# Two-layer hybrid decoder trunk: pairs of feed-forward chunks multiplied by seven block products

## The chip, the cores and the metric

The kernel runs on one NeuronCore of a Trainium2 chip. The metric is the device time of one execution in microseconds. The kernel before took 992.43 us (median of 3 runs, 991.97 to 992.92).

## The reference

The input x is 256 tokens of 1024 values in fp32. Two layers are computed. Each is a feed-forward block, a token mixer and a second feed-forward block, each behind an RMS norm and added to x (the feed-forward blocks with a factor 0.5). The mixer of layer 0 is a causal convolution module (pointwise, gate, 31-tap depthwise, layer norm, pointwise), that of layer 1 is stick-breaking attention with 16 heads of 64. One RMS norm ends it. The part that the change concerns is the feed-forward block:

```python
def swiglu_ffn(h, w_in, w_out):          # h: 256 x 1024, w_in: 1024 x 5632, w_out: 2816 x 1024
    gate, up = jnp.split(h @ w_in, 2, axis=-1)
    return (jax.nn.silu(gate) * up) @ w_out

x = x + 0.5 * swiglu_ffn(rms_norm(x, g[0]), ffn_w_in[i, 0], ffn_w_out[i, 0])
x = x + mixer(rms_norm(x, g[1]))
x = x + 0.5 * swiglu_ffn(rms_norm(x, g[2]), ffn_w_in[i, 1], ffn_w_out[i, 1])
```

There are four such blocks, called the first to the fourth below: the first and the second lie around the convolution, the third and the fourth around the attention.

## The kernel before, in words

**Numbers.** Every large product is made of three matmuls of a reduced fp32 type (fp32r). An operand is split into "hi", a cast copy made by ScalarE, and "lo", the difference that VectorE computes (`split`, L147 to L149); `mm3` (L177) then adds hi x hi, hi x lo and lo x hi into one PSUM bank. Weights arrive by DMA in a raw buffer (pool `rawp`, three of them, each 8 KB a partition) and are split into a pair of hi and lo buffers (pool `ring`, six pairs). `load_w` (L151) does this in pieces of 1024 elements a partition. All weight loads are issued on SP's queue.

**A feed-forward block** (`ffn`, L263) runs over 11 chunks of 256 hidden columns. For a chunk j the kernel loads two weight tiles of w_in (four of the eight 128-row slices each; 256 gate and 256 up columns side by side) and one row tile of w_out (`load_rows`, "v"), computes the up-projection and the gate, and one chunk later adds the chunk's down-projection to four PSUM banks that collect the block's output (`V`, L309, 12 matmuls of 512 columns for each half t of the tokens). There are two forms of the up-projection:
- U (`u_mm`, L227, with `gate`, L267, and `A`, L277): the tokens are the stationary operand and 512 weight columns move. 24 matmuls of 512 columns for each half of 128 tokens. The result has tokens in the partitions; sigmoid and two products follow, then two transposes by TensorE (`A`) and a split.
- C (`C`, L287, with `u_cm`, L235): 128 weight columns are stationary, and the tokens move, hi and lo side by side (512 columns) for the weights' hi and 256 columns for their lo. The result has hidden columns in the partitions and needs no transposes.

The norm's gain is multiplied into the transposed x (`gain`, L203, tile `xg`, 512 elements, tag "B"), which is then split into `xT` (`split_x`, `boundary`, L216). The norm's factor of a token, rstd, is not in `xT`: U's gate multiplies by it, and C multiplies by a row of it (`rrow`, L294 on VectorE, L298 on GpSimd). Chunk 0 of a block, and chunks 0 and 1 of the first, are in the form U, the rest in the form C.

**Order.** The framework in which the kernel is written plans each engine's order before the run: it takes the instructions by program order, as they become ready in its own estimate, and gives out the buffers of a pool as they come free. Each engine then runs its list in order. The opening (`start`, L804) and the convolution (L584 to L647) have their orders written out by hand on TensorE, ScalarE, VectorE and SP. Small work tiles share tags: thirteen buffers of tag "A", four of "B", four each of "H" and "L" for the down-projection's operand.

## Time and profile before

| | before |
|---|---|
| median of 3 runs | 992.43 us (991.97 to 992.92) |
| profiled execution | 992.41 us, span 990.6 us |
| TensorE matmuls | 977.4 us busy (99%), 5658 of them |
| VectorE | 722.3 us busy (73%), 1127 instructions |
| ScalarE | 514.0 us busy (52%), 873 |
| GpSimd | 132.8 us busy (13%), 165 |
| granted TensorE clock | 0.997 of 2.4 GHz (mean) |
| moved from HBM | 171.10 MB, 174 GB/s over the span |

Busy times are sums of recorded durations, and the records of successive instructions of one engine overlap a little: the distance between two starts is shorter than a duration. PE is TensorE's matmul queue, DVE VectorE, ACT ScalarE, POOL GpSimd, SP the engine that issues most DMAs. The blocks lie at about 0 to 205, 306 to 490, 490 to 677 and 797 to 988 us of the span; the convolution is between the first two, attention from 677 to 797.

### The profile page before, as it was taken

How to read it: one execution, taken by the hardware profiler on the slowest of the kernel's cores; microseconds unless marked ns; L12 is line 12 of the kernel's file. 1: busy time of each engine (PE TensorE's matmuls, PEld its weight loads, DVE VectorE, ACT ScalarE, POOL GpSimd, SP SyncE). 2: the span in 40 equal slices, each digit the busy share in tenths (PEclk: the TensorE clock that was granted, in tenths of full speed). 3: DMA queues.
4: the chain of work that ended last, by engine and by line, in shares of the span. 5: the costliest groups of instructions: out<-in, count | busy, mean ns of one | idle time of the engine just before them, and what ended most of it. 6: DMA issues, size and time to landing. Idle time of an engine off the chain costs nothing.

```text
span 990.6 us, 14730 instructions
## 1 busy us (share of the span) xinstructions
PE 977.4 (99%) x5658; PEld 813.6 (82%) x5658; DVE 722.3 (73%) x1127; ACT 514.0 (52%) x873; POOL 132.8 (13%) x165
## 2 busy tenths in 40 slices
PE   8999999999999999999999999999999999999996
PEld 7888888886788888888888888888777688888885
DVE  5886767659869776767876767676867887767654
ACT  6664545355437555455554545454644455554532
POOL 3011111100001111111211111112100011111111
PEclk9999999999999999999999999999999999999998
DMA  7976564447736564646456565654633344646411
GB/s 256 314 242 219 193 228 148 152 125 224 226 96 223 170 229 151 227 155 216 155 192 203 171 211 165 218 152 154 205 126 130 120 153 157 230 151 223 160 43 42
DMA packets 142630, 177.17 MB, mean 179 GB/s; under 512 B 6393, under 2 KB 125792, under 8 KB 142560
## 3 DMA queue, kind: packets, MB, share of 16 engines
q1 hardware_dynamic: 142208, 175.69, 54.5%
q8 instruction: 44, 0.72, 0.3%
q10 hardware_dynamic: 352, 0.55, 0.1%
q14 instruction: 26, 0.21, 0.1%
HBM read 171.10 MB, written 1.05 MB: 174 GB/s over the span
## 4 chain that ended last, share of the span: by engine, by line
PE 92%; DVE 3%; issue 2%; ACT 1%; DMA 1%; POOL 0%; SPq 0%; POOLq 0%; ACTq 0%; DVEq 0%
PE psc L242 28%; PE psc L243 16%; PE psv L178 8%; PE psv L180 8%; PE psv L179 8%; PE psc L245 4%; PE psu L178 3%; PE psu L179 3%; PE psu L180 3%; PE pc L506 3%; DVE lo L149 2%; PE ptr L200 1%; PE pz L700 1%; DMA raw<-in_ffn_w_in_dram 1%; ACT hi L148 1%
## 5 line engine op out<-in xcount | busy, mean ns | idle before, releaser
L149 DVE TENSOR_TENSOR lo<-raw,hi 128x1024 fp32r<-128x1024 f32 (+1 forms) x358 | 398.9, 1137 | 79.4 <-ACT hi L148 79.0
L242 PE MATMUL psc<-xT,hi 128*128 128x512 f32 x1204 | 433.4, 399 | 0.1
L148 ACT CAST hi<-raw 128x1024 fp32r<-128x1024 f32 (+1 forms) x360 | 327.5, 952 | 89.4 <-PE psc L242 34.1
L243 PE MATMUL psc<-xT,lo 128*128 128x256 f32 x1376 | 358.8, 281 | 0.0
L243 PEld LDWEIGHTS psc<-xT,lo 128*128 128x128 f32 x1376 | 260.0, 189 | 15.6 <-issue 0.4
L242 PEld LDWEIGHTS psc<-xT,hi 128*128 128x128 f32 x1204 | 226.6, 188 | 49.3 <-DVE u L248 0.4
L298 POOL TENSOR_TENSOR s<-s,rrow 128x256 f32<-128x256 f32 x78 | 90.7, 1163 | 580.1 <-DVE s L297 580.1
L178 PE MATMUL psv<-hi,ah 128*128 128x512 f32 x354 | 138.2, 390 | 0.3
L179 PE MATMUL psv<-lo,ah 128*128 128x512 f32 x354 | 137.6, 389 | 0.0
L180 PE MATMUL psv<-hi,al 128*128 128x512 f32 x354 | 137.1, 389 | 0.0
L247 ACT COPY u<-psc 128x256 f32<-128x256 f32 x172 | 63.5, 369 | 130.0 <-PE psc L245 129.9
L248 DVE TENSOR_TENSOR u<-psc,u 128x256 f32<-128x256 f32 x172 | 72.5, 421 | 78.4 <-ACT u L247 77.7
L148 ACT CAST ah<-s 128x256 fp32r<-128x256 f32 x78 | 31.7, 407 | 92.2 <-DVE s L300 92.0
L179 PEld LDWEIGHTS psv<-lo,ah 128*128 128x128 f32 x354 | 66.6, 188 | 13.8
L180 PEld LDWEIGHTS psv<-hi,al 128*128 128x128 f32 x354 | 66.4, 188 | 13.8
L178 PEld LDWEIGHTS psv<-hi,ah 128*128 128x128 f32 x354 | 66.5, 188 | 13.3 <-ACT ah L148 1.4
L178 PE MATMUL psu<-hi,xT 128*128 128x512 f32 x176 | 70.2, 399 | 0.2 <-ACT hi L148 0.2
L179 PE MATMUL psu<-lo,xT 128*128 128x512 f32 x176 | 69.3, 394 | 0.8 <-DVE lo L149 0.6
L180 PE MATMUL psu<-hi,xT 128*128 128x512 f32 x176 | 68.9, 391 | 0.0
L245 PE MATMUL psc<-xT,hi 128*128 128x512 f32 x172 | 68.4, 398 | 0.0
L296 ACT ACTIVATE s<-u 128x256 f32<-128x256 f32 x78 | 32.4, 415 | 47.7 <-DVE u L294 47.7
L149 DVE TENSOR_TENSOR al<-s,ah 128x256 fp32r<-128x256 f32 x78 | 33.0, 422 | 21.1 <-ACT ah L148 20.9
(134 smaller groups left out, 800.6 us busy)
## 6 DMA issues: line engine op xcount, KB each, us to landing
raw<-in_ffn_w_in_dram SPq DMA_DIRECT2D x168, 512.0 KB, 4.6
raw<-in_ffn_w_out_dram SPq DMA_DIRECT2D x44, 1024.0 KB, 4.8
raw<-in_conv_w_pw_dram SPq DMA_DIRECT2D x16, 512.0 KB, 4.6
raw<-in_attn_w_qkv_dram SPq DMA_DIRECT2D x16, 512.0 KB, 5.1
raw<-in_ffn_w_in_dram SPq DMA_DIRECT2D x16, 256.0 KB, 5.0
raw<-in_conv_w_pw_dram SPq DMA_DIRECT2D x4, 1024.0 KB, 4.9
raw<-in_attn_w_qkv_dram SPq DMA_DIRECT2D x4, 1024.0 KB, 5.0
raw<-in_attn_w_o_dram SPq DMA_DIRECT2D x4, 1024.0 KB, 4.7
```

Source lines behind the costliest of these rows:

```text
L148: copy(hi, src)
L149: (eng or nc.vector).tensor_tensor(lo, src, hi.bitcast(F32), op=ALU.subtract)
L178: nc.tensor.matmul(ps, lh, rh, start=start, stop=False)
L179: nc.tensor.matmul(ps, lh, rl, start=False, stop=False)
L180: nc.tensor.matmul(ps, ll, rh, start=False, stop=stop)
L242: nc.tensor.matmul(ps, h, xT[:, :, k, :, :], start=k == 0, stop=False)
L243: nc.tensor.matmul(ps[:, :, 0, :], l, xT[:, :, k, 0, :], start=False, stop=False)
L245: nc.tensor.matmul(ps, h, xT[:, :, k, :, :], start=False, stop=True)
L247: nc.scalar.copy(u, ps[:, :, 1, :])
L248: nc.vector.tensor_tensor(u, ps[:, :, 0, :], u, op=ALU.add)
L296: nc.scalar.activation(a, u, AF.Sigmoid)
L298: nc.gpsimd.tensor_tensor(a, a, rrow, op=ALU.mult)
```

## The change

Pairs of chunks (ja, jb) are computed by Strassen's scheme in Winograd's form (`strassen`). The tokens (two halves t) and the contraction (two halves of four 128-row slices) make x a 2 x 2 block matrix, the contraction halves and the two chunks make w_in one. Seven products of 128 tokens x 512 contraction x 512 columns replace eight. Four of the seven weight operands are formed by subtractions in the raw buffers (`less`, in two pieces of 1024), all seven are split (`cast`). Four of the token operands are sums, formed once a block (`normalize`). The products go alternately to two PSUM banks; copies and additions (`keep`, `plus`, 512 elements each) combine them.

As the sums have to be of normalized tokens, `normalize` multiplies the kept `xg` tiles by the row of rstd, splits them into `xT` anew, and from there on the gates need no rstd (`gate_normal`; `C` leaves its two products out). A pair's results go through `gate_normal` and `A`, so that a pair needs four times two transposes.

A plan says what each chunk does: the first block UUCCUnSUUCC, the others UUnUSUSUUUU (U and C as above, n normalize, S a pair). All chunks of the second to fourth block outside of the pairs are in the form U. The waiting down-projections of the chunk before a pair are placed between its products (`later`) and after them; those of a pair come after the next chunk. The convolution's constants are loaded after the first block's chunk 8 instead of chunk 5. There are four raw buffers instead of three and ten work tiles "A" instead of thirteen, and some small tiles share buffers of other tags. The number of hi and lo buffers stays at six.

```diff
@@ -42,7 +42,7 @@
-    rawp = ctx.enter_context(tc.tile_pool(name="rawp", bufs=3))
+    rawp = ctx.enter_context(tc.tile_pool(name="rawp", bufs=4))
...
@@ -59,13 +59,12 @@
-    grow = const.tile([NG, P], F32, name="grow")
+    grow = wk.tile([NG, P], F32, tag="sg", name="grow")
-    vrow = const.tile([NV, P], F32, name="vrow")
...
@@ -215,9 +213,11 @@
 
     def boundary(t, gi):
 
+        xgs = []
         for q in range(2):
-            split_x(t, q, gain(turn_x(t, q), gi, q))
-        return *operand(t), rms_stats(t)
+            xgs.append(gain(turn_x(t, q), gi, q))
+            split_x(t, q, xgs[q])
+        return *operand(t), rms_stats(t), xgs
 
     def u_step(ps, t, k, units):
         h, l = operand(t)
...
@@ -243,7 +243,7 @@
-        u = wk.tile([P, T, P], F32, tag="A", bufs=13, name=nm("u"))
+        u = wk.tile([P, T, P], F32, tag="A", bufs=10, name=nm("u"))
...
@@ -262,15 +262,25 @@
 
     def ffn(i, f, gi, hTs, next_gi, first=None, start=None, hook=None, final=False):
         w_in, w_out = ffn_w_in[i, f], ffn_w_out[i, f]
-        act, aT = {}, {}
+        act, aT, normal, sums = {}, {}, [], []
+
+        def gate_normal(t, j, src):
+
+            s = wk.tile([P, 256], F32, tag="A", bufs=10, name=nm("s"))
+            nc.scalar.activation(s, src[:, 0:256], AF.Sigmoid)
+            nc.vector.tensor_tensor(s, src[:, 0:256], s, op=ALU.mult)
+            nc.vector.tensor_tensor(s, src[:, 256:512], s, op=ALU.mult)
+            act[t, j] = s
 
         def gate(t, j, ps):
+            if normal:
+                return gate_normal(t, j, ps)
             rstd = hTs[t][2]
-            s = wk.tile([P, 256], F32, tag="A", bufs=13, name=nm("s"))
+            s = wk.tile([P, 256], F32, tag="A", bufs=10, name=nm("s"))
             nc.scalar.activation(s, ps[:, 0:256], AF.Sigmoid, scale=rstd)
-            p = wk.tile([P, 256], F32, tag="A", bufs=13, name=nm("p"))
+            p = wk.tile([P, 256], F32, tag="A", bufs=10, name=nm("p"))
             nc.vector.scalar_tensor_tensor(p, ps[:, 0:256], rstd, s, op0=ALU.mult, op1=ALU.mult)
-            a = wk.tile([P, 256], F32, tag="A", bufs=13, name=nm("a"))
+            a = wk.tile([P, 256], F32, tag="A", bufs=10, name=nm("a"))
             nc.vector.scalar_tensor_tensor(a, ps[:, 256:512], rstd, p, op0=ALU.mult, op1=ALU.mult)
             act[t, j] = a
 
...
@@ -291,11 +301,13 @@
                 for c in range(2):
                     u = u_cm([w[:, :, c, q * P : (q + 1) * P] for w in unit] for unit in units)
                     if c == 0:
-                        nc.vector.tensor_tensor(u, u, rrow, op=ALU.mult)
-                        a = wk.tile([P, T, P], F32, tag="A", bufs=13, name=nm("s"))
+                        if not normal:
+                            nc.vector.tensor_tensor(u, u, rrow, op=ALU.mult)
+                        a = wk.tile([P, T, P], F32, tag="A", bufs=10, name=nm("s"))
                         nc.scalar.activation(a, u, AF.Sigmoid)
                         nc.vector.tensor_tensor(a, a, u, op=ALU.mult)
-                        nc.gpsimd.tensor_tensor(a, a, rrow, op=ALU.mult)
+                        if not normal:
+                            nc.gpsimd.tensor_tensor(a, a, rrow, op=ALU.mult)
                     else:
                         nc.vector.tensor_tensor(a, a, u, op=ALU.mult)
                 ah = operands.tile([P, T, P], F32R, tag="H", bufs=4, name=nm("ah"))
...
@@ -305,6 +317,106 @@
                 ls.append(al)
             for t in range(T):
                 aT[t, j] = [h[:, t, :] for h in hs], [l[:, t, :] for l in ls]
+
+        def normalize():
+
+            x11, x12, x21, x22 = (xg for t in range(T) for xg in hTs[t][3])
+            for n, xg in enumerate((x11, x12, x21, x22)):
+                t, q = divmod(n, 2)
+                nc.vector.tensor_tensor(
+                    xg, xg, rrow[:, t, :].unsqueeze(1).broadcast_to([P, 4, P]), op=ALU.mult
+                )
+                split_x(t, q, xg)
+            normal.append(True)
+
+            def operand_of(dst, a, b, op):
+                nc.vector.tensor_tensor(dst, a, b, op=op)
+                hl = wk.tile([P, 2, 4, P], F32R, tag="sk", bufs=4, name=nm("sx"))
+                split(hl[:, 0], hl[:, 1], dst)
+                return hl[:, 0], hl[:, 1]
+
+            s1 = operand_of(x22, x21, x22, ALU.add)
+            s3 = operand_of(x21, x11, x21, ALU.subtract)
+            s2 = operand_of(x11, x22, x11, ALU.subtract)
+            s4 = operand_of(x12, x12, x11, ALU.subtract)
+            sums.extend((s1, s2, s3, s4))
+
+        def strassen(ja, jb, later):
+
+            wv = w_in.rearrange("(k p) n -> p k n", p=P)
+            raw = {}
+            for h, j in ((0, ja), (0, jb), (1, jb), (1, ja)):
+                raw[h, j] = rawp.tile([P, 4, 2, 256], F32, tag="raw", name=nm("raw"))
+                for c in range(2):
+                    c0 = c * DFF + 256 * j
+                    nc.sync.dma_start(raw[h, j][:, :, c, :], wv[:, 4 * h : 4 * h + 4, c0 : c0 + 256])
+            b11, b12, b21, b22 = raw[0, ja], raw[0, jb], raw[1, ja], raw[1, jb]
+            pieces = [slice(0, 2), slice(2, 4)]
+
+            def cast(src):
+                hi, lo = (ring.tile([P, 4, 2, 256], F32R, tag=tag, name=nm(tag)) for tag in ("hi", "lo"))
+                for ks in pieces:
+                    split(hi[:, ks], lo[:, ks], src[:, ks])
+                return hi, lo
+
+            def less(dst, a, b):
+                for ks in pieces:
+                    nc.vector.tensor_tensor(dst[:, ks], a[:, ks], b[:, ks], op=ALU.subtract)
+
+            def product(ps, x, w):
+                for k in range(4):
+                    mm3(ps, x[0][:, k, :], x[1][:, k, :], w[0][:, k], w[1][:, k], k == 0, k == 3)
+
+            def old(t, q):
+                h, l = operand(t)
+                return h[:, 4 * q : 4 * q + 4, :], l[:, 4 * q : 4 * q + 4, :]
+
+            def plus(a, b, dst=None):
+                if dst is None:
+                    dst = wk.tile([P, 512], F32, tag="B", bufs=4, name=nm("sum"))
+                nc.vector.tensor_tensor(dst, a, b, op=ALU.add)
+                return dst
+
+            def keep(src):
+                dst = wk.tile([P, 512], F32, tag="B", bufs=4, name=nm("kept"))
+                nc.scalar.copy(dst, src)
+                return dst
+
+            s1, s2, s3, s4 = sums
+            px, py = (ps_u.tile([P, 512], F32, tag="u", name=nm("psp")) for _ in range(2))
+            w = cast(b11)
+            product(px, old(0, 0), w)
+            less(b11, b12, b11)
+            w = cast(b11)
+            p1 = keep(px)
+            product(py, s1, w)
+            less(b11, b22, b11)
+            w = cast(b11)
+            p5 = keep(py)
+            product(px, s2, w)
+            w = cast(b21)
+            u2 = plus(px, p1)
+            product(py, old(0, 1), w)
+            later(0)
+            less(b12, b22, b12)
+            w = cast(b12)
+            gate_normal(0, ja, plus(py, p1, p1))
+            product(px, s3, w)
+            less(b21, b21, b11)
+            w = cast(b21)
+            u3 = plus(px, u2)
+            plus(u2, p5, u2)
+            product(py, old(1, 1), w)
+            gate_normal(1, jb, plus(u3, p5, p5))
+            w = cast(b22)
+            gate_normal(1, ja, plus(py, u3, u3))
+            product(px, s4, w)
+            gate_normal(0, jb, plus(px, u2, u2))
+            A(0, ja)
+            A(1, jb)
+            later(1)
+            A(1, ja)
+            A(0, jb)
 
         def V(t, j, unit, qs=(0, 1)):
             ah, al = aT[t, j]
...
@@ -370,37 +482,70 @@
             for t in range(T)
         ]
         outs, vus = [None, None], []
-        for j in range(NJ):
-            if j == 0 and first:
-                units = first
-            elif not start or j >= lead:
-                units = load_pairs(w_in, 256 * j, DFF + 256 * j, 256, pieces=2 if j else 4)
-            if j == 0 or j >= lead:
-                vus += [load_rows(w_out, 2 * c) for c in range(len(vus), j + 1)]
-            if j == lead:
+
+        plan = list("UUCCUnSUUCC" if start else "UUnUSUSUUUU")
+        j, waiting, rrow = 0, [], None
+
+        def load_vus(last):
+            vus.extend(load_rows(w_out, 2 * c) for c in range(len(vus), last + 1))
+
+        def finish_waiting():
+            for c, t in waiting:
+                V(t, c, vus[c])
+
+        while j < NJ:
+            kind = plan.pop(0)
+            if j >= lead and rrow is None:
                 rrow = row_rstd(hTs)
-            if j < lead:
-                if not start:
+            if kind == "n":
+                normalize()
+                continue
+            if kind == "S":
+                before = waiting
+
+                def later(t):
+                    for c, tt in before:
+                        if tt == t:
+                            V(t, c, vus[c])
+
+                strassen(j, j + 1, later)
+                load_vus(j + 1)
+                waiting = [(j, 0), (j + 1, 1), (j, 1), (j + 1, 0)]
+                j += 2
+            else:
+                if j == 0 and first:
+                    units = first
+                elif not start or j >= lead:
+                    units = load_pairs(w_in, 256 * j, DFF + 256 * j, 256, pieces=2 if j else 4)
+                if j == 0 or j >= lead:
+                    load_vus(j)
+                if kind == "U":
+                    if j >= lead or not start:
+                        for t in range(T):
+                            gate(t, j, u_mm(t, units))
                     for t in range(T):
-                        gate(t, j, u_mm(t, units))
-                for t in range(T):
-                    A(t, j)
-            else:
-                C(j, units, rrow)
-            if j == NJ - 1:
-                V(0, j - 1, vus[j - 1])
-                V(1, j - 1, vus[j - 1], (0,))
-                V(0, j, vus[j])
-                finish = end_final if final else end
-                outs[0] = finish(0)
-                V(1, j - 1, vus[j - 1], (1,))
-                V(1, j, vus[j])
-                outs[1] = finish(1)
-            elif j:
-                for t in range(T):
-                    V(t, j - 1, vus[j - 1])
-            if j == 5 and hook:
+                        A(t, j)
+                else:
+                    C(j, units, rrow)
+                if j == NJ - 1:
+                    for c, t in waiting:
+                        if c < j - 1:
+                            V(t, c, vus[c])
+                    V(0, j - 1, vus[j - 1])
+                    V(1, j - 1, vus[j - 1], (0,))
+                    V(0, j, vus[j])
+                    finish = end_final if final else end
+                    outs[0] = finish(0)
+                    V(1, j - 1, vus[j - 1], (1,))
+                    V(1, j, vus[j])
+                    outs[1] = finish(1)
+                else:
+                    finish_waiting()
+                    waiting = [(j, t) for t in range(T)]
+                j += 1
+            if hook and j >= 9:
                 hook()
+                hook = None
         return outs
 
 
...
@@ -652,6 +797,8 @@
+        maskn = wk.tile([P, P], BF16, tag="sg", name="maskn")
+        identb = wk.tile([P, P], BF16, tag="sg", name="identb")
```

## Rows read from the trace of the kernel before

**Rows 1.** The page, parts 1 and 2: engine totals, granted clock in 40 slices.
```profile
PE 977.4 (99%) x5658; PEld 813.6 (82%) x5658; DVE 722.3 (73%) x1127; ACT 514.0 (52%) x873; POOL 132.8 (13%) x165
...
PEclk9999999999999999999999999999999999999998
```
**Rows 2.** Waits of TensorE's matmuls: engine, line, releaser, us in total, times, longest.
```profile
PE spare L813 <- POOL ident masks.py:199: 1.7, 1, 1.7
PE pc L506 <- issue: 1.4, 2, 0.8
```
**Rows 3.** Stretch, busy PE, PEld, DVE, ACT, POOL, clock, DMA: opening, block 2, attention, chunk.
```profile
0.00:31.60 31.60, 28.89 (x130) 23.26 (x131) 19.96 (x32) 19.48 (x33) 7.54 (x20) 1.00 0.81 270
...
306.00:490.00 184.00, 183.81 (x961) 156.18 (x960) 136.28 (x209) 99.99 (x162) 25.62 (x23) 1.00 0.59 195
...
677.00:797.00 120.00, 119.06 (x662) 91.64 (x661) 92.95 (x147) 58.62 (x119) 15.73 (x21) 1.00 0.44 141
...
584.75:601.47 16.72, 16.72 (x89) 14.32 (x88) 11.86 (x19) 8.82 (x14) 2.40 (x2) 1.00 0.59 188
```
**Rows 4.** Timeline of TensorE, that chunk: start, duration, engine, line, operation.
```profile
584.75 0.39 PE L242 MATMUL psc<-xT,hi 128*128 128x512 f32 x1
...
596.02 0.40 PE L178 MATMUL psv<-hi,ah 128*128 128x512 f32 x1
...
601.47 0.39 PE L242 MATMUL psc<-xT,hi 128*128 128x512 f32 x1
```
**Rows 5.** The same, end of the third block's U chunk and an A.
```profile
499.11 0.39 PE L178 MATMUL psu<-hi,xT 128*128 128x512 f32 x1
...
500.24 0.39 PE L180 MATMUL psu<-hi,xT 128*128 128x512 f32 x1
500.48 0.38 PE L281 MATMUL ptr<-ident,a 128*128 128x128 f32 x2
500.61 0.48 PE L242 MATMUL psc<-xT,hi 128*128 128x512 f32 x1
500.92 0.28 PE L243 MATMUL psc<-xT,lo 128*128 128x256 f32 x1
```
**Rows 6.** Timeline of VectorE, a block's boundary and a C chunk.
```profile
488.09 1.22 DVE L149 TENSOR_TENSOR lo<-raw,hi 128x1024 fp32r<-128x1024 f32 x1
489.22 0.69 DVE L332 SCALAR_TENSOR_TENSOR x<-psv,x 128x512 f32<-128x512 f32 x1
489.82 0.69 DVE L206 TENSOR_TENSOR xg<-ptr,gvec 128x512 f32<-128x512 f32 x1
...
326.80 0.42 DVE L297 TENSOR_TENSOR s<-s,u 128x256 f32<-128x256 f32 x1
327.13 1.22 DVE L149 TENSOR_TENSOR lo<-raw,hi 128x1024 fp32r<-128x1024 f32 x1
328.27 0.42 DVE L248 TENSOR_TENSOR u<-psc,u 128x256 f32<-128x256 f32 x1
328.60 1.44 DVE L149 TENSOR_TENSOR lo<-raw,hi 128x1024 fp32r<-128x1024 f32 x1
```
**Rows 7.** Groups of instructions by form: count, busy us, mean ns, idle before.
```profile
L149 DVE TENSOR_TENSOR lo<-raw,hi 128x1024 fp32r<-128x1024 f32 x280 | 347.5, 1256 | 73.8 <-ACT hi L148 73.6
```
**Rows 8.** Timeline of ScalarE in a steady chunk: two casts in a row.
```profile
364.96 2.00 ACT L148 CAST hi<-raw 128x1024 fp32r<-128x1024 f32 x2 [0.70 <-PE psv L180]
```
**Rows 9.** Waits of VectorE and ScalarE, the whole span.
```profile
DVE lo L149 <- ACT hi L148: 79.0, 83, 2.4
...
ACT hi L148 <- PE psc L242: 34.1, 36, 1.0
ACT hi L148 <- PE psv L180: 23.8, 33, 1.2
```
**Rows 10.** DMA issues: tile, queue, count, size of each, median us to landing.
```profile
raw<-in_ffn_w_in_dram SPq DMA_DIRECT2D x168, 512.0 KB, 4.6
...
lnb<-in_conv_ln_b_dram SPq DMA_DIRECT2D x1, 512.0 KB, 7.7
```

More of the change, by code (lines that the diff above doesn't have):

```diff
@@ L77, in load_vecs @@
     def load_vecs():
+        vrow = wk.tile([NV, P], F32, tag="sg", name="vrow")
         r0 = 0
@@ L122, in load_conv_consts @@
                 )
-            rowc = wk.tile([P, 32, 4], F32, tag="rowc", name="rowc")
+            rowc = wk.tile([P, 32, 4], F32, tag="B", bufs=4, name="rowc")
             nc.gpsimd.tensor_copy(rowc, rows.rearrange("p i c -> p c i"))
@@ L136, in trunk_kernel @@
     lnb = const.tile([P, D], F32, name="lnb")
-    maskn = const.tile([P, P], BF16, name="maskn")
-    identb = const.tile([P, P], BF16, name="identb")
     uid = [0]
@@ L254, in row_rstd @@
         for t in range(T):
-            rb = wk.tile([P, P], F32, tag="A", bufs=13, name=nm("rb"))
+            rb = wk.tile([P, P], F32, tag="A", bufs=10, name=nm("rb"))
             nc.gpsimd.tensor_copy(rb, hTs[t][2].broadcast_to([P, P]))
@@ L577, in conv @@
         for _ in range(KD):
-            up.append(wk.tile([P, H + T * P], F32, tag="A", bufs=13, name=nm("up")))
+            up.append(wk.tile([P, H + T * P], F32, tag="A", bufs=10, name=nm("up")))
             nc.gpsimd.memset(up[-1][:, :H], 0.0)
@@ L712, in scores @@
                 nc.scalar.activation(be, pz, AF.Sigmoid, scale=scale)
-                sc = wk.tile([P, WS], F32, tag="A", bufs=13, name=nm("scan"))
+                sc = wk.tile([P, WS], F32, tag="A", bufs=10, name=nm("scan"))
                 nc.vector.tensor_tensor_scan(
@@ L716, in scores @@
                 )
-                a = wk.tile([P, 3, P], F32, tag="A", bufs=13, name=nm("aa"))
+                a = wk.tile([P, 3, P], F32, tag="A", bufs=10, name=nm("aa"))
                 nc.vector.tensor_tensor(a[:, 0, :], be[:, 0, :], sc[:, 1 : P + 1], op=ALU.mult)
@@ L730, in transpose_a @@
                     nc.tensor.transpose(pa[:, c, :], a[:, c, :], ident)
-                aT = wk.tile([P, 3, P], F32, tag="A", bufs=13, name=nm("aT"))
+                aT = wk.tile([P, 3, P], F32, tag="A", bufs=10, name=nm("aT"))
                 nc.vector.tensor_copy(aT, pa)
@@ L846, in start @@
             pts = [turn_x(0, q) for q in range(2)]
-            xgs = [gain(pts[q], 0, q) for q in range(2)]
+            first_xgs = [gain(pts[q], 0, q) for q in range(2)]
             for q in range(2):
-                split_x(0, q, xgs[q])
+                split_x(0, q, first_xgs[q])
             keep_busy(8)
@@ L867, in start @@
             rstds.append(rms_stats(1))
-            hTs.extend((*operand(t), rstds[t]) for t in range(T))
+            hTs.extend((*operand(t), rstds[t], (first_xgs, xgs)[t]) for t in range(T))
             mm(0, (1, 3), (0, 4))
```

## The prediction

> **What bounds the kernel now.** I read the page's engine totals first, then the waits of the matmul engine, the busy time by stage, and the timelines of TensorE, VectorE and ScalarE inside one steady chunk. TensorE is busy 977.4 of 990.6 us at full granted clock [rows 1]. It hardly waits: the largest wait behind the opening one is 1.4 us [rows 2]. In a whole block it idles 0.2 of 184 us, and in one steady chunk of 16.72 us not at all, while VectorE is busy 11.86 us and ScalarE 8.82 us of it [rows 3]. So whatever takes matmul time away shortens the run, as long as VectorE, the next engine, still delivers its operands in time. Both sides have to be counted.
>
> **What the pairs remove from TensorE.** A C chunk runs its up-projection from 584.75 to 596.02, 11.27 us, and its down-projection (24 matmuls of 512 columns) to 601.47, 5.45 us, 0.227 each [rows 4]. In the U form the same 512-column matmuls follow each other at 1.13/5 = 0.226 us; two fp32 transposes take 0.13 us and make the next matmul 0.31 instead of 0.23 long, 0.21 us for each A in all [rows 5]. I use 0.2265 us per matmul.
> - A pair now: 2 x 11.27 = 22.54 us of up-projection. After: 7 products x 4 slices x 3 matmuls = 84 x 0.2265 = 19.03, plus 4 A's x 0.21 = 0.84, together 19.87 us. Saved: 2.67 us a pair. The down-projection stays at 10.9 us.
> - There are 1 + 2 + 2 + 2 = 7 pairs: -18.7 us.
> - Other chunks go from C to U: three in the first block, six in each of the others, 21 in all. U costs 48 x 0.2265 + 2 x 0.21 = 11.29 us, so +0.02 each, +0.4 us.
> Sum on TensorE: -18.3 us, if no wait arises.
>
> **What the change puts on VectorE.** Back to back, a 1024-element operation starts 1.13 to 1.14 us after the one before, a 512 one 0.60, a 256 one 0.33 to 0.34; their durations in the record are 1.22, 0.69 and 0.42 [rows 6]. A pair has 14 "lo" halves of seven operands, 8 subtractions that form four of the weight operands, 4 "lo" halves of two row tiles, 7 additions of 512 and 12 operations of 256 (eight in the gates, four in the A's): 26 x 1.14 + 7 x 0.60 + 12 x 0.34 = 37.9 us. Two C chunks need 12 x 1.14 + 24 x 0.34 = 21.8. TensorE has 19.9 + 10.9 = 30.8 us for a pair, so inside one VectorE is short; over a block it is not: 7 U chunks x 8.9 + 2 x 37.9 + 16 x 0.60 for the normalization = 148 us, against 7 x 16.7 + 2 x 30.8 = 179 on TensorE. The question is whether VectorE's lead carries it over the pairs.
>
> The lead that a pair needs: up to the seventh operand's first half VectorE has 22 x 1.14 + 5 x 0.60 + 4 x 0.34 - 1.14 = 28.3 us to do; TensorE in that time runs six products (2.72 each) and one down-projection of the waiting chunk (2.72), 19.0 us. Needed: 9.3 us, or 6.6 if the second waiting half is moved ahead as well.
> The lead that it gets:
> - Blocks two to four, first pair. Between the end of U(1) and the pair TensorE has V(0), U(2), V(1), 22.2 us. VectorE has the rest of the normalization (its multiplications and the first rows' split can run beside U(1); two splits, four sums and their splits are left, 10 x 0.60) and 8 gate and A operations x 0.34: 8.7 us. So 13.5 us remain, which is four operands with two subtractions; the six buffer pairs allow it, since V(0) and U(2) hand theirs back before the pair. 4 us too much: no stall.
> - Second pair. From product 7 of the first pair to the next: 2.7 (P7) + 2.7 + 11.3 + 10.9 = 27.6 us on TensorE; VectorE has the tail of the pair and ten row and U halves, 18.4 us. 9.2 us, plus what was left over: no stall.
> - First block. The pair follows the normalization directly. Two operands with two subtractions ahead make 9.1 us; normalization and U(4)'s gates take 7.4, of which V(3) covers 5.45. 7.1 us are left against 9.3 needed, or 6.6: a stall of 0 to 2.2. I take 2.
> Only two PSUM banks serve the products, so product n+2 waits until VectorE or ScalarE has emptied product n's bank, and that read can stand behind one 1.14 us operation. Between no delay and 1.14 us once a pair I take 0.5 a pair where VectorE keeps up: 6 x 0.5 = 3 us.
>
> The Trainium skill ("VectorE: DVE Perf Modes", Terms) says that the pipeline is flushed after every VectorE operation and the next cannot issue until it is empty, and (The TRN2 errata) gives an fp32 tensor_tensor (N + 151)/0.96 ns, which is 1.22 us at 1024. The trace's durations agree, its start-to-start does not: 1.13 to 1.14 [rows 6]. What a pair would cost if durations counted is the first rival below.
>
> **The other edits.**
> - ScalarE: 18 casts at 0.95 us in a row [rows 8], two copies, four sigmoids and four A copies are some 21.5 us in a pair's 30.8: hidden; it issues in order, so a cast that waits for a subtraction holds the copies that empty banks (inside the 0.5).
> - The multiplications on GpSimd go for all but four chunks; beside one a 1024 operation took 1.44 us, and the mean of 280 is 1.256 [rows 6, 7]. That gives VectorE a little back, nothing to TensorE.
> - All four raw buffers are held by a pair. The next loads start when the fifth operand is cast, over 10 us before v of the next tiles is wanted; a load lands 4.6 us after its issue [rows 10]. Hidden by products 6 and 7; with that cover gone it would be one landing a pair.
> - The fourth raw buffer lets the opening's last load go early; TensorE idles 2.7 us in the first 31.6 [rows 3], 1.7 of them before its first matmul [rows 2]: -1.0 to 0. I take 0.
> - The convolution's constants are loaded after chunk 8 instead of chunk 5, through SP's queue. Their issues stand between the weight loads, and the rows wait for shared buffers. The slowest took 7.7 us to land [rows 10]. Two chunks (33 us) lie between: 0; up to +8 if the queue is held.
> - Ten work tiles instead of thirteen: only attention keeps many, and TensorE idles 0.9 of 120 us there [rows 3]. 0 to +1; I take 0.
>
> **The sum.** The profiled execution took 992.41 us (span 990.6 and 1.8 around it), the median of the runs is 992.43, so one figure serves both. 992.4 - 18.3 = 974.1; plus 2 and 3 of stalls: 979 us, 1.4% less.
>
> **The rivals.**
> 1. VectorE is occupied for the whole recorded duration. Then the lead needed is 22 x 1.22 + 5 x 0.69 + 4 x 0.42 - 1.2 - 19.0 = 11.8; got are 11.9 (first pair), 7.0 (second), 6.7 (first block): stalls 0, 4.8, 5.1, in all 3 x 4.8 + 5.1 = 19.5. 974.1 + 19.5 = 994 us: the gain is eaten up. By the flush rule of the Trainium skill's VectorE page this is what would come. For it: every record's length; against it: the starts [rows 6].
> 2. Slower: VectorE's in-order queue pays for the cast chain. Each operand goes VectorE (subtract), ScalarE (hi), VectorE (lo), and VectorE waits for ScalarE once an operand. Now it waits there 83 times, 79.0 us, 0.95 each [rows 9]. With w per operand the need grows by 7w, the lead of a second pair shrinks by 5w, that of the first block by 2w; at w = 0.95 the stalls are 2.5 (first pair), 11.5 (second) and 10.8 (first block): 3 x 14.0 + 10.8 = 53 us, 1027 us. It decides from w = 0.43, where the stalls reach 18.3. For it: the waits are there now, and the chain gets one link longer. Against it: ScalarE waits 34.1 and 23.8 us for the matmuls that free its buffers [rows 9], so most of VectorE's waits are that of an engine that is ahead, and two halves that follow each other show 2.00 us on ScalarE without a gap [rows 8].
> 3. The covers hold better than I say and the opening gains its 1 us: 973 us.
> That the saving doesn't arise at all (the order of the instructions puts no down-projection between the products, and every shortage shows) is inside rival 1's price.
>
> **Chances.** Forecast (972 to 986) 0.62; rival 1 (986 to 998) 0.18, of which half is still faster; rival 2 (above 998) 0.15; rival 3 below 972, 0.05. A measurement of this kernel tells 0.2%, 2 us, from no change. Faster: 0.62 + 0.05 + 0.09 = 0.76; within 0.2%: 0.07, from rival 1's middle; slower: 0.02 + 0.15 = 0.17. The range reaches from 970 (no stall and the opening's gain, with the matmul time 2 us off over 7 pairs) to 998 (rival 1 with the 0.5's on top). The likeliest case's own range is 972 to 986.
>
> **What would show it.** Products at 0.227 us per matmul, 2.72 us apart; VectorE without a pause in the pairs, with starts 1.14 us apart; TensorE's idle time in a block under 3 us, and ahead of P6 and P7 if anywhere. Wrong would be: TensorE waiting on "lo" of the subtracted operands for over 2.7 us a pair, idle stretches in which the granted clock falls, or attention longer than its 120 us.

## The result, and the profile after

The changed kernel took 981.75 us (median of 4 runs, 980.99 to 984.91) against 992.67 us (991.97 to 993.19) for the kernel before on the same chip: a ratio of 0.9896, 95% interval 0.9874 to 0.9919. A second measurement of it, of five runs, gave 982.06 us and 0.9900 (0.9885 to 0.9915). The forecast was 979 us in 970 to 998. The profiled execution took 981.38 us, 979.6 of it span and 1.8 around it, 11.0 less than the profiled one before.

The page of the changed kernel, the lines that answer to [rows 1]:

```profile
PE 964.9 (98%) x5154; PEld 780.6 (80%) x5154; DVE 800.0 (82%) x1124; ACT 526.0 (54%) x821; POOL 46.3 (5%) x91
...
PEclk9999999999999999999999999999999999999999
```

TensorE lost 12.5 us of busy time and VectorE gained 78. Span minus busy time of TensorE is 14.7 us, before it was 13.2: the missing part of the forecast's 18.3 us is not idle time. It is in the length of the matmul stream itself.

The windows of both kernels, cut where the first matmul of each block (or of the stage behind it) starts; the columns are those of [rows 3]. First before, in the order first block with opening, convolution, second block, third, attention, fourth:

```profile
0.00:197.24 197.24, 194.28 (x997) 163.33 (x997) 144.55 (x227) 108.69 (x180) 30.57 (x52) 1.00 0.66 220
197.24:302.11 104.87, 103.43 (x1076) 81.43 (x1073) 79.86 (x129) 48.76 (x90) 4.07 (x13) 1.00 0.51 160
302.11:489.00 186.89, 186.70 (x977) 158.57 (x976) 139.17 (x212) 102.88 (x167) 27.56 (x27) 1.00 0.60 197
489.00:675.53 186.53, 186.46 (x978) 158.62 (x976) 136.46 (x210) 100.24 (x163) 28.36 (x27) 1.00 0.58 186
675.53:797.97 122.44, 121.50 (x677) 93.61 (x676) 95.39 (x151) 60.70 (x121) 15.73 (x21) 1.00 0.44 141
797.97:990.60 192.63, 185.00 (x971) 158.04 (x969) 126.89 (x204) 92.70 (x156) 26.47 (x26) 0.99 0.44 146
```

The same six stages of the changed kernel:

```profile
0.00:195.39 195.39, 192.53 (x925) 158.58 (x925) 157.49 (x230) 112.55 (x176) 13.69 (x34) 1.00 0.66 227
195.39:301.48 106.09, 103.05 (x1075) 81.16 (x1073) 79.89 (x129) 48.95 (x90) 3.71 (x12) 1.00 0.51 159
301.48:484.85 183.37, 183.15 (x833) 149.10 (x832) 160.58 (x210) 105.83 (x151) 3.68 (x7) 1.00 0.59 201
484.85:667.67 182.82, 182.82 (x833) 149.38 (x832) 158.07 (x208) 102.76 (x147) 5.87 (x12) 1.00 0.57 190
667.67:790.17 122.50, 121.61 (x677) 93.63 (x676) 95.33 (x151) 60.71 (x121) 15.74 (x21) 1.00 0.44 140
790.17:979.60 189.43, 181.70 (x827) 148.71 (x825) 148.63 (x202) 95.18 (x140) 3.57 (x6) 0.99 0.42 143
```

The gain is 1.85 us in the block with one pair and 3.52, 3.71 and 3.20 in those with two. The convolution gave 1.22 back, attention is as it was. In the third block TensorE is busy for 182.82 of 182.82 us: not one visible wait, with VectorE at 158.

One pair and the U chunk behind it (first line), and a U chunk by itself (second), in the third block after:

```profile
530.78:578.93 48.15, 48.15 (x218) 39.33 (x216) 46.92 (x58) 28.53 (x38) 0.00 (x0) 1.00 0.57 197
627.07:643.98 16.91, 16.91 (x77) 13.79 (x76) 10.22 (x15) 7.39 (x12) 0.00 (x0) 1.00 0.61 188
```

48.15 - 16.91 = 31.24 us is a pair with its down-projections. Two C chunks took 2 x 16.72 = 33.44 [rows 3]: 2.20 saved, where 2.67 was forecast. A U chunk costs 0.19 more than a C chunk, where 0.02 was forecast. VectorE is busy in 46.92 of the pair's and its neighbour's 48.15 us and TensorE still does not wait.

The waits of TensorE's matmuls after (columns of [rows 2]; psu is the bank of a U chunk's up-projection, psp that of a pair's products, psv that of the down-projections, ptr that of transposes, pc that of the convolution's taps):

```profile
PE pc L651 <- issue: 3.0, 2, 2.4
...
PE psu L177 <- DVE lo L147: 0.5, 2, 0.3
```

In the blocks behind the opening nothing over 0.3 us at a time is left in this profile; the largest wait is that of the taps.

### The profile page after: what moved, and what is told of

It is laid out like the page before. It is cut to its first block, busy times and chain, and to the rows that moved or that the text cites. A ratio compares the mean times of both kernels' runs of the same rounds, so it can differ in the third digit from the quotient of the medians.

```text
span 979.6 us, 13642 instructions
## 1 busy us (share of the span) xinstructions
PE 964.9 (98%) x5154; PEld 780.6 (80%) x5154; DVE 800.0 (82%) x1124; ACT 526.0 (54%) x821; POOL 46.3 (5%) x91
## 4 chain that ended last, share of the span: by engine, by line
PE 94%; DVE 2%; DMA 1%; ACT 1%; issue 1%; SPq 0%; POOLq 0%; ACTq 0%; DVEq 0%
PE psu L177 12%; PE psu L178 12%; PE psu L176 12%; PE psv L178 9%; PE psv L177 9%; PE psv L176 9%; PE psc L242 5%; PE psp L176 4%; PE psp L177 4%; PE psp L178 4%; PE psc L243 3%; PE pc L651 3%; PE ptr L291 2%; DMA raw<-in_ffn_w_in_dram 1%; PE ptr L198 1%; PE pz L847 1%
## 5 line engine op out<-in xcount | busy, mean ns | idle before, releaser
L176 PE MATMUL psu<-hi,xT 128*128 128x512 f32 x512 | 200.5, 394 | 0.2 <-ACT hi L146 0.2
L177 PE MATMUL psu<-lo,xT 128*128 128x512 f32 x512 | 199.5, 392 | 0.9 <-DVE lo L147 0.5
L178 PE MATMUL psu<-hi,xT 128*128 128x512 f32 x512 | 199.8, 391 | 0.0
L177 PEld LDWEIGHTS psu<-lo,xT 128*128 128x128 f32 x512 | 96.2, 188 | 21.5 <-DVE lo L147 1.4
L176 PEld LDWEIGHTS psu<-hi,xT 128*128 128x128 f32 x512 | 96.0, 188 | 20.7 <-issue 1.2
L178 PEld LDWEIGHTS psu<-hi,xT 128*128 128x128 f32 x512 | 96.2, 188 | 19.5
L242 PE MATMUL psc<-xT,hi 128*128 128x512 f32 x224 | 81.3, 401 | 0.0
L176 PEld LDWEIGHTS psv<-hi,ah 128*128 128x128 f32 x354 | 66.6, 188 | 12.5 <-ACT ah L146 0.2
L364 DVE TENSOR_TENSOR raw<-raw,raw 128x1024 f32<-128x1024 f32 x56 | 67.2, 1215 | 0.0
L243 PE MATMUL psc<-xT,lo 128*128 128x256 f32 x256 | 66.9, 282 | 0.0
L243 PEld LDWEIGHTS psc<-xT,lo 128*128 128x128 f32 x256 | 48.3, 189 | 3.0 <-issue 0.4
L242 PEld LDWEIGHTS psc<-xT,hi 128*128 128x128 f32 x224 | 42.1, 188 | 9.4 <-ACT vs L830 0.3
L176 PE MATMUL psp<-hi,sx 128*128 128x512 f32 x112 | 44.3, 396 | 0.0
```

The costliest lines, as they stand in the source:

```text
L176: nc.tensor.matmul(ps, lh, rh, start=start, stop=False)
L177: nc.tensor.matmul(ps, lh, rl, start=False, stop=False)
L178: nc.tensor.matmul(ps, ll, rh, start=False, stop=stop)
L242: nc.tensor.matmul(ps, h, xT[:, :, k, :, :], start=k == 0, stop=False)
L243: nc.tensor.matmul(ps[:, :, 0, :], l, xT[:, :, k, 0, :], start=False, stop=False)
L364: nc.vector.tensor_tensor(dst[:, ks], a[:, ks], b[:, ks], op=ALU.subtract)
```

## The experiments

The plan string of `ffn` makes most of them one-line edits. Each was timed against the kernel before on the same chip.

**1. No pairs.** Everything else of the change stays: normalization, sums, buffers, late constants.

```diff
-        plan = list("UUCCUnSUUCC" if start else "UUnUSUSUUUU")
+        plan = list("UUCCUnCCCCCC" if start else "UUnCCCCCCCCC")
```

> No pairs: every chunk behind the normalization is in the form C, the rest of the change (normalization, four raw buffers, ten work tiles, late constants) stays. Theory (the gain is TensorE's columns saved in the pairs): the gain is gone, 994.5 us: the 992.4 of before, 0.2 for each of the four chunks that become U and 1.2 for the longer convolution seen after the change. Rival (the gain comes from the buffers and from the rstd products taken off VectorE and GpSimd): 981 to 985 us.

994.03 us against 991.40, ratio 1.0025 (1.0014 to 1.0037). The whole gain is the pairs'; the rest of the change costs 2.6 us. By stages the cost lies in the convolution (107.52 us against 104.87 before; the four blocks together are 0.3 shorter than before, so the 0.2 for each added U chunk did not show). TensorE's wait for the taps is there without any pair:

```profile
PE pc L651 <- issue: 3.2, 1, 3.2
```

At the end of that wait the granted clock fell: over the convolution it averaged 0.98 in this profile, and TensorE was busy for 104.3 us there, against 103.1 in the changed kernel.

**2. C chunks outside of the pairs.**

```diff
-        plan = list("UUCCUnSUUCC" if start else "UUnUSUSUUUU")
+        plan = list("UUCCUnSCCCC" if start else "UUnCSCSCCCC")
```

> The same seven pairs, but the chunks behind the normalization that are not in pairs are in the form C instead of U (17 chunks). After the change a U chunk took 16.91 us against 16.72 for a C chunk before. Theory (TensorE's work sets the time, and an A costs 0.27 us and not 0.21): 17 x 0.19 = 3.2 us less than the changed kernel, 978 us, TensorE's idle time in the blocks under 1 us. Rival (VectorE is close to its limit; C gives it 1.3 us more a chunk): TensorE waits at the pairs, 982 us or more.

982.12 us, ratio 0.9901 (0.9881 to 0.9922): no gain, the expectation failed. An undisturbed C chunk is again 16.72 us long, but the pair with the C behind it takes 48.29 (578.60 to 626.89) against 48.15 with a U. TensorE's busy time stayed at 964.8 us and VectorE's rose to 825.7. So 0.19 a chunk is only gained away from pairs. By stages, the four blocks together are 0.5 us shorter than in the changed kernel instead of 3.2 (the fourth is 1.1 longer, with 1.5 us more of idle time), and the two stages that the edit does not touch got longer: the convolution by 1.1 us (the wait for the taps is 4.0 in all) and attention by 1.6. In attention the granted clock was at its lower level (0.50 of 2.4 GHz) for a stretch:

```profile
767.36:770.77 3.41, 3.41 (x13) 2.64 (x11) 1.79 (x5) 0.94 (x3) 0.00 (x0) 0.50 0.94 277
```

TensorE had no wait over 0.2 us in the 20 us before that stretch, so what made the clock fall is open. The profiled execution took 983.67 us, the longest of the four runs, and (5) has the same in attention while no other profile has, so these 1.6 us need not be the edit's.

**3. Three pairs in a block instead of two.**

```diff
-        plan = list("UUCCUnSUUCC" if start else "UUnUSUSUUUU")
+        plan = list("UUCCUnSUUCC" if start else "UUnSUSUSU")
```

> Three pairs instead of two in the second to fourth block (plan UUnSUSUSU; the first block as it is). A pair took 31.24 us of TensorE where two U chunks take 33.82. Theory (VectorE needs 46.8 us for a pair and a U chunk, TensorE has 48.15, so its lead comes back in each round): 3 x 2.6 = 7.7 us less than the changed kernel, 974 us. Rival (the lead is used up by the second pair and the third one stalls by 2.6 us or more): 981 us or more, with waits ahead of the third pair's subtracted operands.

984.46 us, ratio 0.9922 (0.9898 to 0.9945): the rival's side. The interval overlaps that of the changed kernel; the 7.7 us did not come. The profile is of the fastest of the four runs, 981.75 us. The third block in a window, then the waits of TensorE's matmuls over the whole span:

```profile
484.68:668.00 183.32, 181.51 (x822) 146.88 (x819) 177.27 (x229) 109.28 (x155) 5.00 (x12) 1.00 0.57 190
```

```profile
PE psu L176 <- ACT hi L146: 3.3, 4, 1.2
...
PE psv L177 <- DVE lo L147: 1.4, 3, 0.6
```

VectorE is busy for 177.27 of 183.32 us: the budget is used up. The third pair should have taken 2 x 16.91 - 31.24 = 2.58 us off the block; busy time fell by 1.31 and 1.81 us of idle time came. The stall came in the first round, at the end of the pair that stands directly behind the normalization, and not at the third pair, as the rival had put it. That VectorE has no chunk there behind which it can run ahead is argued, not shown: the first block's pair also follows its normalization and waited no more than 0.25 us in the changed kernel, but it has five chunks in front of it, and this one two.

**4. The two pairs back to back.** The same work in another order.

```diff
-        plan = list("UUCCUnSUUCC" if start else "UUnUSUSUUUU")
+        plan = list("UUCCUnSUUCC" if start else "UUnUSSUUUU")
```

> The two pairs of the second to fourth block follow each other with no U chunk between (plan UUnUSSUUUU): the same TensorE work as the changed kernel, but VectorE has no time to get ahead of the second pair. Theory (VectorE's lead carries a pair; it needs 6.5 us here, or 1.1 if the waiting down-projections are moved ahead, and has none): TensorE stalls 1 to 6.5 us in each of three blocks, 985 to 1001 us. Rival (no lead is needed, VectorE keeps up inside a pair): as the changed kernel, 981 to 982 us.

991.09 us, ratio 0.9997 (0.9982 to 1.0012): 9.3 us above the changed kernel's 981.75, within the expected range, and the gain is gone. Of these the order of the pairs costs about 8: the three blocks that the edit touches got longer by 2.36, 3.01 and 2.64 us. Another 2.0 are in the first block, which is unedited; its 197.38 us are near the 197.04 of a second profile of the changed kernel, and both have a wait of 1.3 to 1.4 us at about 35 us. The waits of TensorE's matmuls:

```profile
PE psu L176 <- ACT hi L146: 2.7, 4, 1.1
PE psv L177 <- DVE lo L147: 2.2, 6, 0.6
```

They stand at the end of the second pair: in the third block at 593.2 (the first matmul of the U chunk behind the products) and at 595.2 and 597.4 (its down-projections). Of the 8.0 us in the three blocks 4.8 are idle time and 3.2 longer busy time, at a mean granted clock of 0.998 as in the changed kernel: a stall costs more than its idle time.

**5. The sums in another pool.** The tiles of the sums (and what shares their buffers) are allocated from the pool of xT.

```diff
-                hl = wk.tile([P, 2, 4, P], F32R, tag="sk", bufs=4, name=nm("sx"))
+                hl = operands.tile([P, 2, 4, P], F32R, tag="sk", bufs=4, name=nm("sx"))
...
```

> The split sums (tile sx) lie in the pool of the token operands instead of the work pool; nothing else changes. In the changed kernel a product whose stationary operand is a sum ran at 233.5 ns a matmul, one whose stationary operand is xT at 227. Theory A (where the stationary operand lies in SBUF sets the pace): the four products with sums run at 227 too, 7 x 48 x 6.5 ns = 2.2 us less. Theory B (the pace goes with what VectorE and ScalarE do beside those products): still 233, and the time is that of the changed kernel.

981.24 us, ratio 0.9886 (0.9866 to 0.9907); by time alone not to be told from the changed kernel. The trace can tell it: over all 315 steps inside products with a sum as stationary operand, the mean start-to-start fell from 233.5 to 230.6 ns (those with xT: 228.1 and 227.6), a little under half of the expected effect. In this profile attention took 124.03 us instead of 122.50, with a stretch at the lower clock as in (2), which hides as much. The mean hides several levels. Timeline of TensorE, the product with the third sum (s3 of the tokens) in the second block, then in the third:

```profile
359.72 0.39 PE L176 MATMUL psp<-hi,sx 128*128 128x512 f32 x1
...
362.44 0.39 PE L176 MATMUL psp<-hi,xT 128*128 128x512 f32 x1
...
542.14 0.41 PE L176 MATMUL psp<-hi,sx 128*128 128x512 f32 x1
...
544.70 0.40 PE L178 MATMUL psp<-hi,sx 128*128 128x512 f32 x1
```

The first runs at 2.72/12 = 227 ns, the second at 2.56/11 = 233 ns a matmul. The operation is the same, and what is known to differ is the buffers. The paces repeat: in the second block the products with the four sums run at 229.1, 232.8, 226.6 and 233.5 ns in the first pair and at 229.2, 233.0, 226.8 and 233.6 in the second. In the changed kernel all 28 lie between 232.8 and 234.5. So the pace goes with where the tile lies, and theory B, which put it down to what VectorE and ScalarE do beside, is not needed. What about the place decides stays open.

**6. The fourth raw buffer held back in the convolution.** A tile of that pool is taken at the stage's start and released by a small copy that reads the taps' last sum (acc[7]), so that the 1 MB load of the next block does not get ahead of the last tap copies in SP's queue.

```diff
+        hold = rawp.tile([P, 4, 2, 256], F32, tag="raw", name="hold")
+        nc.gpsimd.memset(hold[:, 0, 0, 0:1], 0.0)
...
+            nc.gpsimd.tensor_copy(hold[:, 0, 0, 0:1], acc[7][:, T * P - 1 : T * P])
```

> The fourth raw buffer is held from the convolution's start to its last taps, so that no weight load of the next block can be issued into it while the convolution shifts its input by small DMAs. In the changed kernel a 1 MB load went out at 256.7 us ahead of eight of these copies, which landed at 265 to 267 us, and the taps waited 2.4 us. Theory (that load is why the convolution got 1.2 us longer): the wait falls to the 0.8 us of before and the time by 1 to 2 us. Rival (the copies are late for the earlier issue of everything or the later constants): the wait stays, same time.

980.67 us (978.75 to 980.93), ratio 0.9876 (0.9857 to 0.9895). The interval overlaps that of the changed kernel, so the traces have to tell. DMA issues on SP's queue, first in the changed kernel, then with the buffer held (start, duration, line, tile):

```profile
255.27 1.13 SPq L564 DMA_DIRECT2D raw<-in_ffn_w_in_dram  x2
256.74 0.37 SPq L155 DMA_DIRECT2D raw<-in_ffn_w_out_dram  x1
257.80 7.83 SPq L641 DMA_DIRECT2D sk<-up  x8
```

```profile
256.69 1.61 SPq L564 DMA_DIRECT2D raw<-in_ffn_w_in_dram  x2
258.39 6.16 SPq L641 DMA_DIRECT2D sk<-up  x8
264.65 0.55 SPq L155 DMA_DIRECT2D raw<-in_ffn_w_out_dram  x1
```

And how long these eight copies took to land, the changed kernel first:

```profile
sk<-up SPq DMA_DIRECT2D x8, 64.0 KB, 7.3
```

```profile
sk<-up SPq DMA_DIRECT2D x8, 64.0 KB, 3.8
```

Behind a load of 1 MB the copies of 64 KB took 7.3 us, without it 3.8. In all nine profiles that have the load ahead of them the median is 5.2 to 7.8 us; with the buffer held it is 3.8 here and 4.5 in (9). That the load delays the copies is shown. The Trainium skill ("DMA: Bandwidth & Descriptors", Queues, rings and completion order) says that each engine takes a ring's descriptors in the order of the ring; the landing times fit that, but a load that only shares the engines with the copies could delay them too.

What the delay costs is less clear. Here the wait of the taps fell from 3.0 us to 0.2 (1.1 at the transposes of the same stage came in part in its place), and the stage from 106.09 to 103.94. But with the load ahead the wait was anything from 0.7 us (5) to 4.0 (2), and with the buffer held in (9) it was 1.7, and the stage no shorter than in a second profile of the changed kernel, the first line below:

```profile
197.04:302.05 105.01, 103.06 (x1076) 81.17 (x1074) 79.91 (x129) 48.99 (x90) 3.73 (x12) 1.00 0.52 160
```

```profile
193.35:298.43 105.08, 103.18 (x1076) 81.30 (x1074) 80.79 (x131) 48.91 (x90) 3.92 (x13) 1.00 0.57 180
```

**7 and 8. Scrap work on VectorE.** `less` is called four times a pair. Behind every second call one more subtraction of 1024 elements into a tile that nobody reads (7, two a pair), or behind every call two (8, eight a pair; `range(2)` in the place of `range(len(calls) % 2)`).

```diff
+            calls = []
...
             def less(dst, a, b):
+                calls.append(1)
                 for ks in pieces:
                     nc.vector.tensor_tensor(dst[:, ks], a[:, ks], b[:, ks], op=ALU.subtract)
+                for _ in range(len(calls) % 2):
+                    junk = wk.tile([P, D], F32, tag="sc4", name=nm("junk"))
+                    nc.vector.tensor_tensor(junk, xt[0], xt[1], op=ALU.subtract)
```

> Two more 1024-element subtractions into a scrap tile on VectorE in each pair, 2.3 us a pair and 16 us in all. Theory (VectorE's lead covers a pair with some 4 us to spare): no more than 3 us longer than the changed kernel, mostly from the first block. Rival (VectorE sets the time inside the pairs): 2.3 us a pair, 16 us longer, 997 us.

> Eight more such subtractions in each pair, 9.1 us a pair and 64 us in all. Theory (4 us to spare in each pair, and a pair and a U chunk need 46.8 of 48.2 us): 4 to 8 us longer a pair, 28 to 55 us in all, 1010 to 1035 us. Rival (there is far more to spare than I count): under 10 us longer.

Two a pair, 14 x 1.14 = 16 us in all: 982.45 us, ratio 0.9899 (0.9882 to 0.9915), 0.7 us above the changed kernel. Eight a pair, 64 us: 1023.55 us, ratio 1.0312 (1.0286 to 1.0338), 41.8 more. So in the changed kernel VectorE has over 2 us to spare in a pair and under 9. Waits of TensorE with eight a pair, and a window over a pair of the third block:

```profile
PE psv L176 <- ACT hi L146: 9.5, 4, 2.9
PE psp L176 <- ACT hi L146: 3.5, 3, 1.2
```

```profile
574.00:645.00 71.00, 64.20 (x265) 49.35 (x264) 67.60 (x83) 35.93 (x49) 1.40 (x5) 0.95 0.52 171
```

Of the 42 us only 22.8 are idle time of TensorE (1021.9 - 984.4 against 14.7); 19.5 are longer busy time. In that window the engine idled 6.8 us, and the granted clock averaged 0.95, so part of the stretch ran at the lower of its two levels (1.2 GHz); over the run its mean was 0.986, against 0.998 in the changed kernel. An estimate from these two: 0.012 x 1021.9 = 12 of the 19.5 us are the lower clock's.

**9. What the experiments point to.** The buffer held as in 6, the sums placed as in 5, and a second pair in the first block.

```diff
-        plan = list("UUCCUnSUUCC" if start else "UUnUSUSUUUU")
+        plan = list("UUCCUnSUSU" if start else "UUnUSUSUUUU")
```

> The changed kernel with the held raw buffer, the sums in the pool of the token operands, and a second pair in the first block (plan UUCCUnSUSU). Theory (a pair that has a U chunk ahead of it saves 2.4 us on TensorE and costs no wait): the convolution back at 104 us (-2.1), products with sums at 230.5 ns (-1.0), the first block 2.2 us shorter: 976 us. Rival (the convolution's constants, now behind the second pair, or the thinner lead in the first block take it back): 978 us or more.

976.79 us (975.46 to 979.56), ratio 0.9850 (0.9829 to 0.9870); the changed kernel beside it on the same chip 982.06 (980.88 to 983.76).

> The changed kernel as it is, beside the version above on the same chip: 981 to 982 us if its earlier runs stand.

The first block of the better kernel with the opening, in a window:

```profile
0.00:193.35 193.35, 190.44 (x889) 155.59 (x889) 172.44 (x241) 116.06 (x176) 13.63 (x35) 1.00 0.64 219
```

The second pair there stands behind a U chunk. The block is 2.04 us shorter than in the first profile of the changed kernel (195.39) and 3.69 shorter than in the one beside it (197.04, which has the wait of 1.4 us named in 4). The sum of the terms came out, but not every term: the first block gives 3.7 of the 5.3 us between these two profiles, the three others 0.32, 0.39 and 0.95, and the convolution, which was to give 2.1, nothing (105.08 against 105.01).

## Why the prediction was right, and where its terms were off

**The bound.** TensorE's stream is what counts: with the pairs taken out the gain is gone (1), and 16 us more on VectorE cost 0.7 (7).

**TensorE's sum, forecast -18.3, came to -11.4** (7 x 2.20 saved, 21 x 0.19 lost; by the stages the four blocks are 12.3 us shorter). Two terms were too small:
- An A was priced at 0.21 us from one instance [rows 5]. From the whole U chunk it is (16.91 - 72 x 0.227)/2 = 0.28. The price counted the transposes and the matmul behind them only; the same row from start to start, 500.92 - 500.24 - 2 x 0.2265, gives 0.23. Timeline of TensorE after, two places where an A's transposes stand:

```profile
637.72 0.39 PE L178 MATMUL psu<-hi,xT 128*128 128x512 f32 x1
637.95 0.38 PE L291 MATMUL ptr<-ident,s 128*128 128x128 f32 x2
638.09 0.48 PE L176 MATMUL psv<-hi,ah 128*128 128x512 f32 x1
638.40 0.39 PE L177 MATMUL psv<-lo,ah 128*128 128x512 f32 x1
...
639.79 0.39 PE L177 MATMUL psv<-lo,ah 128*128 128x512 f32 x1
640.06 0.41 PE L291 MATMUL ptr<-ident,s 128*128 128x128 f32 x2
640.23 0.47 PE L178 MATMUL psv<-hi,al 128*128 128x512 f32 x1
640.54 0.39 PE L176 MATMUL psv<-hi,ah 128*128 128x512 f32 x1
```

The first A adds 638.40 - 637.72 - 2 x 0.227 = 0.23 us. The second stands inside a down-projection, also delays the start of its own transposes, and adds 0.30. Between them the six steps of the down-projection take 1.39 us, 0.232 each; over the kernel, two successive matmuls of a down-projection start 228.6 ns apart on average, against 227.2 before. There are 70 more A's: 70 x 0.07 = 4.9 us.
- All 84 matmuls of a pair were priced at 0.2265. Timeline of TensorE after, a product with xT and one with a sum:

```profile
579.15 0.39 PE L177 MATMUL psp<-lo,xT 128*128 128x512 f32 x1
...
580.97 0.39 PE L176 MATMUL psp<-hi,xT 128*128 128x512 f32 x1
...
581.65 0.39 PE L176 MATMUL psp<-hi,sx 128*128 128x512 f32 x1
...
583.99 0.39 PE L177 MATMUL psp<-lo,sx 128*128 128x512 f32 x1
```

Eight steps take 1.82 us, 0.2275 each; ten with the sum 2.34, 0.234 each. Four products of 12 in seven pairs: 336 x 6.5 ns = 2.2 us. The two terms make 7.1; the shortfall is 6.9, or 6.0 by the stages.

**The stalls, forecast 5 us, are about 0.** The reasoning on VectorE's lead holds in its order of size: the spare of the pairs lies between 2 and 9 us by (7) and (8), and with the second pair put directly behind the first the stall comes (4). The first block's 2 us and the 0.5 a pair for the banks did not show: no wait there is over 0.3 us. That the two errors have opposite signs, -5 and +6.9, is why the total missed by only 2.75 us, and that is luck: the path was right, and two of its sizes were not.

**Rival 1, durations count, is refuted.** Timeline of VectorE after, in a pair:

```profile
581.07 1.22 DVE L364 TENSOR_TENSOR raw<-raw,raw 128x1024 f32<-128x1024 f32 x1
582.21 1.22 DVE L147 TENSOR_TENSOR lo<-raw,hi 128x1024 fp32r<-128x1024 f32 x1
583.34 1.22 DVE L364 TENSOR_TENSOR raw<-raw,raw 128x1024 f32<-128x1024 f32 x1
584.48 1.22 DVE L147 TENSOR_TENSOR lo<-raw,hi 128x1024 fp32r<-128x1024 f32 x1
```

The starts are 1.13 to 1.14 us apart at 1.22 us of duration, with a subtraction between two splits too. The Trainium skill ("VectorE: DVE Perf Modes", Two Vector instructions with no wait between them) says that a held instruction starts only when every earlier one has finished, and that the groups of partitions at which the instructions read and write decide which one is held. All of these use the full 128 partitions, and none waited for the end of the one in front: the trace agrees with that section, and not with the flush behind every operation that the Trainium skill tells of under Terms.

**Rival 2, the cast chain, is refuted too**, by the wait that was its evidence [rows 9]; VectorE's waits after:

```profile
DVE lo L147 <- ACT hi L146: 49.5, 34, 3.2
```

It fell from 79.0 us in 83 waits, and the time is 981.75 us and not 1027. That fits an engine that had been ahead when it waited for the casts, and now has less time to be ahead in.

**The other edits, forecast 0, cost 1.2 us in this profile**, in the convolution (0.1 in the second profile of the same kernel, 2.6 in (1)). The prediction gave the fourth raw buffer -1 to 0 and the queue's risk to the late constants. The buffer let a load of 1 MB into SP's queue ahead of the taps' copies, and they landed later for it (6); whether it is the whole of the cost is not shown, since holding the buffer made the stage 2.15 us shorter in (6) and no shorter in (9). The opening, attention and the loads inside the pairs came out as said.

## What to carry to other kernels

Price a matmul saving with the whole of the chunk that takes the new form (here 16.91 us against 16.72), not with one instance of the new operation: transposes slow the stream around them. Work moved to a second engine was free here as long as its budget per block and its lead at each place both sufficed; the order alone was worth 8 us. Look at the stages that an edit does not touch: in (2) and (5) attention alone was 1.5 us longer than in the other profiles. One more buffer also moves the transfers that wait for it forward: look for what is queued behind them.

## What the runs showed of the hardware

- The same kind of matmul runs at 227, 229 or 233 ns a piece depending on which buffer its stationary operand lies in (5). The cause is open.
- When TensorE is starved, its busy time grows along with its idle time: 3.2 us beside 4.8 in the three blocks of (4), at the full granted clock; 19.5 beside 22.8 in (8), where by the estimate above the lower clock makes some 12 of it. At the lower level (1.2 GHz) two matmuls of 512 columns started 0.43 us apart (577.91 and 578.34 in (8)), at the higher 0.227.
- Eight copies of 64 KB landed 5.2 to 7.8 us after their issue (medians of nine profiles) with a load of 1 MB ahead of them in the same queue, and 3.8 and 4.5 us without it (6, 9).
